# An even layer planned with new ranks and a new clock model, its queries stacked for the score products, and an odd layer with its first LayerNorm placed later

## The chip, the cores and the metric

The kernel runs on one core of a Trainium2 chip. The metric is the time of one execution on the device in microseconds, the median of repeated runs. The engines' short names are those of the profile: PE is TensorE's matmul stream and PEld its weight loads, DVE is VectorE, ACT is ScalarE, POOL is GpSimd, and SP is the engine that issues nearly all DMAs. "L446" is line 446 of the kernel's file.

## The reference

An encoder of two post-norm layers on x of 512 positions by 1024 features, in fp32, each layer followed by a convolutional FFN. The even layer (cut):

```
z = x @ w_in
q, k, v, u = jnp.split(z, [ATTN_WIDTH, ATTN_WIDTH + KV_WIDTH, ATTN_WIDTH + 2 * KV_WIDTH], axis=-1)
y_attn = windowed_gqa(q, k, v, sink)     # 8 heads of 64, 2 key/value heads, |t - s| <= 128, sink logits, ALiBi
y_s5 = s5_mixer(u, ...)                  # diagonal complex state space, both directions, then GELU and GLU
return jnp.concatenate([y_attn, y_s5], axis=-1) @ w_out
```

The odd layer is a bidirectional mLSTM with 8 heads of 128. Its tail, per head:

```
num = einsum('bhcts,bhcse->bhcte', s, v) + inter[..., None] * einsum('bhctd,bhcde->bhcte', q, c_in)
h = num / jnp.maximum(jnp.abs(den), jnp.exp(-m_t))[..., None]
h = h_fwd + h_bwd
mu = h.mean(-1, keepdims=True); var = jnp.mean(jnp.square(h - mu), -1, keepdims=True)
h = (h - mu) * lax.rsqrt(var + LN_EPS) * norm_g
h = h * jax.nn.sigmoid(o)
return h @ w_out
```

## The kernel before, in words

Every fp32 product is made of three: an operand is split into a high part (a copy rounded to the type fp32r) and a low part (the rest), and `mm3` (L545 to 547) multiplies high by high, low by high and high by low. `nat_tile` (L569) does the same for the products whose result has positions on the partitions.

The even layer, about the first 208 us, is not issued as it is written. The functions `e_*`, `att_*` and `s_*` record their instructions in a `Plan` as steps, with a part name each (`self.plan.part`: "att3", "in2", "pv0"), and `Plan.order` puts all steps of all engines in one order: among those that could start soonest it takes the one of the highest rank, where rank is the weighted length of the chain behind a step (`WEIGHT`, per engine) plus a number for its part (`BIAS`). To know what could start, it goes by costs of its own: `cost` for an instruction, `HOP` between engines, `TURN` between the kinds of products on TensorE, and a rule for TensorE's clock. `Plan.issue` then issues them in that order, so that all of them carry the one line L446 of the profile. What the names in a row say: `xh`, `xl` are the parts of x transposed; `t` is a pool of tiles of 512 columns (pieces of x, parts of q and k, inputs' products); `s` holds scores; `pT` transposed weights of attention; `mh`, `ml` the parts of the mixer's result; `wl` low parts of weights; `E`, `C`, `c`, `U`, `T`, `S`, `So`, `ra`, `rb`, `zx`, `Y` belong to the state space layer, which goes in four blocks of channels: input products (in0 to in3, into banks `b` from `U` and `nU`), rotations (`s_rot`, ending in `S`), output tables (`C`, two buffers), lags, output products (y0 to y3, from `So` and `U` with `C` and `T`), and act (GELU) with its parts. `U` is loaded per block by a DMA into one of two buffers.

Attention: `e_q` projects two heads' queries at once into 128 rows and keeps a high and a low tile of them. `e_kv` keeps k's parts per key head, `kh` and `kl`, each twice: once in its own 64 rows and once copied to the other 64, so that a head in either half of q finds its keys in its own rows. `att_scores` multiplies 64 rows of each with `mm3`, for 16 pairs of head and half, a range of 256 and one of 384 columns each.

The odd layer (`odd`) is issued through the scheduler of the framework as it is written, in steps per head: "q" and "k" (projections with their convolution), "1" (`m_weights`: scores of the head, multiplied by W, the decay matrices, L1541 and 1542), "2" (`m_sum`: the sums over W and v, L1555 and 1557, divided and put together as `hn`, then its LayerNorm, L1573 to 1579), "3" (`m_out`: transposes of `hn`, output gate). The order at its start is "1" of head 0, "q" of head 2, "2" of head 0, "1" of head 1, then "k" of head 2, "2" of head 1, "3" of head 0. LayerNorm's power -1/2 runs on POOL (L1577, `hrs`), which also makes the masked rows `nm` for `m_weights` (L1525) and, for 22 of the weight units, the low part `wl` (L529).

## Time and profile before

| | us |
|---|---|
| median of 3 runs | 1279.37 (1277.39 to 1280.87) |
| the profiled execution | 1279.63 |
| its span (first to last instruction) | 1277.8 |
| mean granted clock of TensorE in it | 0.986 |

The rows below come from the one profiled execution; its span lies 1.83 us under its own time. In the views by stretch, a busy time of an engine is followed by its number of instructions, and PEclk is the granted clock of TensorE as a share of full speed (1.00 is 2.4 GHz, 0.50 is 1.2 GHz). In a timeline, the time in brackets is the idle time of the engine ahead of the row, with what ended it.

### The profile page before, as it was taken

The numbers are of one execution on the slowest core, as the hardware profiler recorded it, in microseconds if no ns is written. First come the engines' busy times: TensorE is split into PE (matmuls) and PEld (weight loads), VectorE is DVE, ScalarE is ACT, GpSimd is POOL, SyncE is SP. The second block draws the span as 40 slices with busy tenths as digits, with TensorE's granted clock in tenths as the row PEclk, the third lists the DMA queues.
The fourth block names the chain that finished last, engine by engine and source line by source line (L and its number), as shares of the span: only waits on it lengthen the run. The fifth ranks groups of instructions, "written<-read, shape, count | busy, mean of one in ns | idle before, by whom it ended". The sixth has DMA issues, their size and how long they took to land.

```text
span 1277.8 us, 17609 instructions
## 1 busy us (share of the span) xinstructions
PE 1243.6 (97%) x6878; PEld 1044.5 (82%) x6878; DVE 718.6 (56%) x1398; ACT 527.4 (41%) x900; POOL 139.5 (11%) x139
## 2 busy tenths in 40 slices
PE   7898999999999999999999999999999999999997
PEld 5776787888888888888888898988988888888886
DVE  7999984764442444425775647375854422544415
ACT  5346765343321243322364746553443321333301
POOL 2013510000000000000014345310000000000000
PEclk9989889999999999999999999999999999999999
DMA  8633533353333233322033232224443321433201
GB/s 252 183 106 107 171 107 102 151 167 115 95 88 99 89 109 99 99 80 86 25 117 105 82 95 76 90 66 132 129 135 100 99 88 61 148 99 97 91 28 66
DMA packets 57459, 135.31 MB, mean 106 GB/s; under 512 B 13888, under 2 KB 22928, under 8 KB 56736
## 3 DMA queue, kind: packets, MB, share of 16 engines
q1 hardware_dynamic: 57376, 134.19, 33.9%
q8 instruction: 54, 0.88, 0.3%
q14 instruction: 29, 0.24, 0.1%
HBM read 129.19 MB, written 4.98 MB: 105 GB/s over the span
## 4 chain that ended last, share of the span: by engine, by line
PE 83%; DVE 9%; DMA 3%; issue 2%; ACT 2%; SPq 1%; POOL 0%; DVEq 0%; POOLq 0%; ACTq 0%
PE b L569 23%; PE b L545 18%; PE b L546 18%; PE b L547 17%; PE b L446 4%; PE b L1555 1%; PE b L1557 1%; DVE t L446 1%; DMA t<-xT_dram 1%; DVE C L446 1%; SPq L446 1%; DMA st<-w_dram 1%; DMA zx<-DZ 1%; DVE s L446 1%; DVE wl L446 0%
## 5 line engine op out<-in xcount | busy, mean ns | idle before, releaser
L545 PE MATMUL b<-xh,wh 128*128 128x512 f32 (+1 forms) x944 | 357.6, 380 | 0.5 <-ACT xh L627 0.5
L546 PE MATMUL b<-xl,wh 128*128 128x512 f32 (+1 forms) x944 | 357.2, 379 | 0.4 <-DVE xl L628 0.3
L547 PE MATMUL b<-xh,wl 128*128 128x512 f32 (+1 forms) x944 | 357.0, 378 | 0.0
L528 ACT CAST wh<-st 128x1024 fp32r<-128x1024 f32 x175 | 183.5, 1052 | 414.5 <-DMA st<-w_dram 146.2
L529 DVE TENSOR_TENSOR wl<-st,wh 128x1024 fp32r<-128x1024 f32 x153 | 188.2, 1232 | 292.6 <-ACT wh L528 288.8
L546 PEld LDWEIGHTS b<-xl,wh 128*128 128x128 f32 x944 | 177.6, 188 | 33.6 <-DVE xl L628 1.1
L547 PEld LDWEIGHTS b<-xh,wl 128*128 128x128 f32 x944 | 177.6, 188 | 33.3
L545 PEld LDWEIGHTS b<-xh,wh 128*128 128x128 f32 x944 | 177.1, 188 | 33.4 <-ACT xh L627 1.0
L569 PE MATMUL b<-wh,hh 128*128 128x512 f32 x352 | 109.3, 390 | 0.0
L569 PE MATMUL b<-wl,hh 128*128 128x512 f32 x352 | 109.2, 389 | 0.0
L569 PE MATMUL b<-wh,hl 128*128 128x512 f32 x352 | 109.2, 389 | 0.0
L610 POOL TENSOR_TENSOR lnrs<-lnsq,mhalf 128x1 f32<-128x1 f32 x16 | 9.7, 606 | 836.1 <-DVE lnsq L609 836.1
L569 PEld LDWEIGHTS b<-wh,hl 128*128 128x128 f32 x352 | 66.1, 188 | 13.8
L569 PEld LDWEIGHTS b<-wl,hh 128*128 128x128 f32 x352 | 66.1, 188 | 13.7
L569 PEld LDWEIGHTS b<-wh,hh 128*128 128x128 f32 x352 | 65.9, 188 | 13.5
L734 DVE TENSOR_TENSOR c<-c,b 128x512 f32<-128x512 f32 x44 | 30.2, 687 | 65.5 <-PE b L547 64.8
L733 ACT ACTIVATE c<-c 128x512 f32<-128x512 f32 x44 | 27.8, 632 | 81.0 <-DVE c L732 81.0
L529 POOL TENSOR_TENSOR wl<-st,wh 128x1024 fp32r<-128x1024 f32 x22 | 52.5, 2392 | 56.4 <-ACT wh L528 53.5
L591 DVE SCALAR_TENSOR_TENSOR x<-x,b 128x512 f32<-128x512 f32 x48 | 31.2, 684 | 43.0 <-PE b L569 39.8
L446 PE MATMUL b<-xh,wh 128*128 128x512 f32 x80 | 32.3, 408 | 7.4 <-ACT xh L446 7.4
L446 ACT ACTIVATE s<-s,m 128x384 f32<-128x384 f32 (+3 forms) x64 | 33.7, 557 | 13.2 <-DVE m L446 12.9
L607 ACT ACTIVATE lnjk<-x,lnmu 128x1024 f32<-128x1024 f32 x16 | 18.4, 1153 | 49.9 <-DVE lnmu L606 49.9
(330 smaller groups left out, 1867.5 us busy)
## 6 DMA issues: line engine op xcount, KB each, us to landing
st<-w_dram SPq DMA_DIRECT2D x192, 512.0 KB, 3.6
tb<-s5bT_dram SPq DMA_DIRECT2D x16, 256.0 KB, 4.3
zx<-DZ SPq DMA_DIRECT2D x16, 256.0 KB, 5.0
lngb<-ln_dram SPq DMA_DIRECT2D x4, 1024.0 KB, 5.6
nb<-DN SPq DMA_DIRECT2D x16, 256.0 KB, 3.8
t<-xT_dram SPq DMA_DIRECT2D x8, 256.0 KB, 5.4
T<-DK SPq DMA_DIRECT2D x32, 64.0 KB, 2.3
x<-x_dram SPq DMA_DIRECT2D x1, 2048.0 KB
```

Source lines behind the costliest of these rows:

```text
L446: getattr(getattr(nc, s.eng), s.name)(*real(s.args), **real(s.kw))
L528: nc.scalar.copy(out=h, in_=x)
L529: eng.tensor_tensor(out=l, in0=x, in1=h.bitcast(F32), op=ALU.subtract)
L545: mm(ps, lhsT=lh, rhs=rh, start=first, stop=False)
L546: mm(ps, lhsT=lh, rhs=rl, start=False, stop=False)
L547: mm(ps, lhsT=ll, rhs=rh, start=False, stop=last)
L569: mm(acc[h], lhsT=hx[:, tok], rhs=wx[:, 512 * h:512 * h + 512], start=a, stop=b)
L591: self.nc.vector.scalar_tensor_tensor(out=xr, in0=xr, scalar=scale, in1=acc[h], op0=ALU.mult, op1=ALU.add, **kw)
L607: nc.scalar.activation(out=jk, in_=x, func=AF.Square, bias=mu, accum_out=sq)
L733: nc.scalar.activation(out=c, in_=c, func=AF.Gelu_apprx_tanh)
L734: nc.vector.tensor_tensor(out=c, in0=c, in1=pg, op=ALU.mult)
L1555: nc.tensor.matmul(pn[:, 0:130], lhsT=Ws[j][:, i - j, :], rhs=va[:, j, h % 2, 0:130], start=j == 0, stop=j == i)
```

## The change

Five things are edited. First, the table of ranks (`BIAS`, `WEIGHT`), of which the diff shows a line. Second, what the planner believes of TensorE: the costs of a turn between kinds of products, and its rule for the clock, which now counts columns instead of costs, with other bounds. Third, `e_kv`: the copy of k's low part to the other 64 rows moves from VectorE to ScalarE. Fourth, `e_q` and `att_scores`: instead of a high and a low tile of both heads, there are two tiles, one per head, with the head's high part in its own 64 rows and its low part in the other 64. Since `kh` holds the same keys in both halves, one product over 128 rows gives high by high and low by high together, and a second one over 64 rows with `kl` the rest. Fifth, in the odd layer the LayerNorm of `m_sum` becomes a function of its own, `m_norm`; it follows `m_sum` at once for all heads but head 0, whose LayerNorm now comes after "1" of head 1.

```diff
-BIAS = {"act0": -6545, "act1": -21250, "act2": -210, "act3": 869, "att0": 17397, "att1": -8738, "att2": 28314,
+BIAS = {"act0": -15215, "act1": -28185, "act2": -8486, "act3": 16119, "att0": 13532, "att1": -8687, "att2": 14400,
...
-WEIGHT = dict(tensor=564.3857644116506, vector=0.10825561484528345, scalar=16158.12505118024, gpsimd=1.858247289234654, sync=0.07166590488045835, form=59.399941409009884)
+WEIGHT = dict(tensor=6921.451288255964, vector=0.09311711213243236, scalar=23712.06630937233, gpsimd=391.23029167485606, sync=0.7156231908378619, form=4.460256149243044)
...
-    TURN = {"FR": 0.22, "FT": 0.18, "RF": 0.15, "RT": 0.05, "TF": 0.145, "TR": 0.105}
+    TURN = {"FR": 0.23, "FT": 0.2, "RF": 0.15, "RT": 0.1, "TF": 0.19, "TR": 0.105}
...
+            wide = math.prod(args[1].shape[1:]) if name == "transpose" else math.prod(kw["rhs"].shape[1:])
+            s.act = wide / 2400 * (2 if name == "transpose" else 1 if kw["rhs"].f32r else 4)
...
-                busy += cost
+                busy += s.act
...
-            nc.vector.tensor_copy(out=kl[kv][other, :], in_=kl[kv][own, :].bitcast(F32))
+            nc.scalar.copy(out=kl[kv][other, :], in_=kl[kv][own, :].bitcast(F32))
...
-        qh = self.t(ap, [P, S], "t", F32R, bufs=NT)
-        ql = self.t(ap, [P, S], "t", F32R, bufs=NT)
-        nc.scalar.activation(out=qh, in_=pq, func=AF.Copy, scale=0.125)
-        nc.vector.scalar_tensor_tensor(out=ql, in0=pq, scalar=0.125, in1=qh.bitcast(F32), op0=ALU.mult, op1=ALU.subtract)
-        return qh, ql
+
+        q = [self.t(ap, [P, S], "t", F32R, bufs=NT) for _ in range(2)]
+        for r in range(2):
+            own, other = slice(64 * r, 64 * r + 64), slice(64 - 64 * r, 128 - 64 * r)
+            nc.scalar.activation(out=q[r][own, :], in_=pq[own, :], func=AF.Copy, scale=0.125)
+            nc.vector.scalar_tensor_tensor(out=q[r][other, :], in0=pq[own, :], scalar=0.125, in1=q[r][own, :].bitcast(F32), op0=ALU.mult, op1=ALU.subtract)
+        return q
...
-            self.mm3(pt[:, 0:n], qh[rows, ds128(j)], ql[rows, ds128(j)], kh[rows, keys], kl[rows, keys], True, True)
+
+            nc.tensor.matmul(pt[:, 0:n], lhsT=q[par][:, ds128(j)], rhs=kh[:, keys], start=True, stop=False)
+            nc.tensor.matmul(pt[:, 0:n], lhsT=q[par][rows, ds128(j)], rhs=kl[rows, keys], start=False, stop=True)
...
+        return hn, st, mv, rs
+
+    def m_norm(self, hn, st, mv, rs):
+        nc = self.nc
+        v = nc.vector
         for i in range(4):
             v.bn_stats(out=st[:, i, :], in_=hn[:, i, :])
...
                 hn[h] = self.m_sum(mp, h, Ws.pop(h), va[h // 2])
+                if h > 0:
+                    hn[h] = self.m_norm(*hn[h])
...
         step("2", 0)
         step("1", 1)
+        hn[0] = self.m_norm(*hn[0])
```

How the order moves is shown at three places. The first is the start of SP's queue, from its first or second transfer of x on. Here `t` is a piece of x, `st` a staged weight, `KS` the small parameters of the state space layer, `tb` its tables. Before:

```order
L446 DMA t_108<-xT_dram 128x512
L446 DMA t_112<-xT_dram 128x512
L446 DMA KS_115<-s5s_dram 128x96
L446 DMA t_118<-xT_dram 128x512
L446 DMA bias_122<-bias_dram 128x384
L446 DMA t_124<-xT_dram 128x512
L446 DMA ident_72<-ident_dram 128x128
L446 DMA pv_73<-pv_dram 128x256
L446 DMA tb_128<-s5bT_dram 128x1x512
L446 DMA DG_130<-dg_dram 80x256
L446 DMA t_132<-xT_dram 128x512
L446 DMA t_134<-xT_dram 128x512
```

After (rows 2 to 13 of SP's order; row 1 is the first piece of x):

```order
L451 DMA t_97<-xT_dram 128x512
L451 DMA st_101<-w_dram 128x1024
L451 DMA st_105<-w_dram 128x1024
L451 DMA t_109<-xT_dram 128x512
L451 DMA t_112<-xT_dram 128x512
L451 DMA t_115<-xT_dram 128x512
L451 DMA t_118<-xT_dram 128x512
L451 DMA KS_122<-s5s_dram 128x96
L451 DMA bias_124<-bias_dram 128x384
L451 DMA t_126<-xT_dram 128x512
L451 DMA ident_72<-ident_dram 128x128
L451 DMA t_129<-xT_dram 128x512
```

Ahead of these stand the two weights and two pieces of x in the order before, and one piece of x in the order after. All eight pieces are issued by the 13th place now, by the 16th before.

The second place is TensorE's, where the input products of block 2 begin (`U_1507` and `U_1641` are that block's U). `b<-t,t` are score products (the parts of k first, of q second), `b<-ident,s` transposes of scores, `b<-pT,t` the products with v, `b<-So,C` output products of block 0 (into `b_1391` in the order after). Before:

```order
L446 MATMUL b_1545<-t_484,t_1044 128x384
L446 MATMUL b_1550<-t_484,t_1044 128x256
L446 MATMUL b_1545<-t_515,t_1044 128x384
L446 MATMUL b_1550<-t_515,t_1044 128x256
L446 MATMUL b_1545<-t_484,t_1066 128x384
L446 MATMUL b_1550<-t_484,t_1066 128x256
L446 MATMUL b_1561<-ident_72,s_1374 128x128 x3
L446 MATMUL b_1430<-pT_1548,t_944 64x128 x3
L446 MATMUL b_1576<-U_1507,t_371_1180 64x64 x2
```

After:

```order
L451 MATMUL b_1567<-pT_1630,t_789 64x128 x3
L451 MATMUL b_1391<-So_1106,C_432 64x64
L451 MATMUL b_1663<-ident_72,s_1509 128x128 x2
L451 MATMUL b_1391<-So_1106,C_432 64x64
L451 MATMUL b_1567<-pT_1665,t_789 64x128 x2
L451 MATMUL b_1391<-So_1106,C_432 64x64
L451 MATMUL b_1681<-ident_72,s_1509 128x128 x3
L451 MATMUL b_1391<-So_1106,C_432 64x64
L451 MATMUL b_1694<-t_499,t_1344 128x384
L451 MATMUL b_1699<-t_499,t_1344 128x256
L451 MATMUL b_1694<-t_514,t_1344 128x384
L451 MATMUL b_1702<-U_1641,t_371_1103 64x64 x2
```

A score has two products where it had three, and the last output products of block 0 (`b_1391`) now stand right ahead of block 2's input, where they were over some rows earlier; the new U takes the buffer that these read.

The third place is VectorE's, in the odd layer, from the LayerNorm of head 0 (`hst`, `hmv`, `hrs`, `hn`) to the products with W of head 1. Before:

```order
L1573 BN_STATS hst_6104<-hn_6103 128x6 x4
L1575 BN_AGGR hmv_6105<-hst_6104 128x2 x4
L1541 TENSOR_TENSOR W_6137<-W_6137,b_6138 128x512
L1576 TENSOR_SCALAR hrs_6106<-hmv_6105 128x4
L1542 TENSOR_TENSOR W_6137<-W_6137,b_6138 128x128
L1579 TENSOR_SCALAR hn_6103<-hn_6103,hmv_6105,hrs_6106 128x128 x4
L1541 TENSOR_TENSOR W_6149<-W_6149,b_6150 128x384
L1542 TENSOR_TENSOR W_6149<-W_6149,b_6150 128x256
L1541 TENSOR_TENSOR W_6161<-W_6161,b_6162 128x256
L1542 TENSOR_TENSOR W_6161<-W_6161,b_6162 128x384
L1541 TENSOR_TENSOR W_6173<-W_6173,b_6174 128x128
L1542 TENSOR_TENSOR W_6173<-W_6173,b_6174 128x512
```

After (the same functions stand some lines lower in the changed file):

```order
L1550 TENSOR_TENSOR W_6099<-W_6099,b_6100 128x128
L1549 TENSOR_TENSOR W_6111<-W_6111,b_6112 128x384
L1550 TENSOR_TENSOR W_6111<-W_6111,b_6112 128x256
L1549 TENSOR_TENSOR W_6123<-W_6123,b_6124 128x256
L1586 BN_STATS hst_6080<-hn_6079 128x6 x3
L1550 TENSOR_TENSOR W_6123<-W_6123,b_6124 128x384
L1549 TENSOR_TENSOR W_6135<-W_6135,b_6136 128x128
L1586 BN_STATS hst_6080<-hn_6079 128x6
L1588 BN_AGGR hmv_6081<-hst_6080 128x2 x4
L1550 TENSOR_TENSOR W_6135<-W_6135,b_6136 128x512
L1589 TENSOR_SCALAR hrs_6082<-hmv_6081 128x4
L1592 TENSOR_SCALAR hn_6079<-hn_6079,hmv_6081,hrs_6082 128x128 x4
```

The statistics, and above all the four normalising steps of `hn` that wait for POOL's `hrs`, stood between the first and the second W; they now stand behind all four.

## Rows read from the trace of the kernel before

**Rows 1.** The page's first part: busy time, share of the span, instructions.

```profile
PE 1243.6 (97%) x6878; PEld 1044.5 (82%) x6878; DVE 718.6 (56%) x1398; ACT 527.4 (41%) x900; POOL 139.5 (11%) x139
```

**Rows 2.** By stretch: length, then PE, PEld, DVE, ACT, POOL, PEclk, DMA, GB/s.

```profile
0.00:20.00 20.00, 11.16 (x37) 8.24 (x38) 12.46 (x43) 9.87 (x13) 7.41 (x15) 1.00 0.92 302
20.00:192.60 172.60, 160.01 (x1493) 129.52 (x1492) 160.12 (x436) 99.15 (x223) 40.50 (x58) 0.91 0.47 137
65.00:75.00 10.00, 10.00 (x103) 9.04 (x102) 7.86 (x19) 3.72 (x11) 1.25 (x1) 0.54 0.30 91
155.00:170.00 15.00, 15.00 (x92) 12.51 (x93) 10.71 (x22) 7.41 (x20) 6.49 (x11) 0.62 0.28 85
208.00:684.60 476.60, 474.27 (x2284) 399.59 (x2283) 238.73 (x353) 170.37 (x234) 17.80 (x17) 1.00 0.33 104
```

**Rows 3.** Timeline at the planned part's end: start us, us, engine, line, operation, count.

```profile
182.54 1.28 ACT L446 ACT_TABLE_LOAD   x1
...
191.30 1.29 DVE L446 TENSOR_TENSOR S<-S,ra 128x512 f32<-128x512 f32 x2
...
198.70 0.50 PE L446 MATMUL b<-xh,ml 128*128 128x512 f32 x1
...
208.19 0.39 PE L545 MATMUL b<-t,wh 128*128 128x512 f32 x1
```

**Rows 4.** Timeline of VectorE: two of its waits in the planned part.

```profile
15.98 0.69 DVE L446 TENSOR_TENSOR xl<-t,xh 128x512 fp32r<-128x512 f32 x1 [1.56 <-ACT xh L446]
...
166.93 2.48 DVE L446 TENSOR_TENSOR C<-bc,b 128x512 f32<-128x512 f32 x4 [3.21 <-PE b L446]
```

**Rows 5.** Timeline of TensorE: waits ahead of two stretches, and score products around one.

```profile
64.23 0.90 PE L446 MATMUL b<-t,t 64*128 64x384 f32 x2 [1.79 <-DVE t L446]
...
146.53 1.15 PE L446 MATMUL b<-t,t 64*128 64x384 f32 x6
...
152.98 1.11 PE L446 MATMUL b<-pT,t 128*64 128x128 f32 x6 [2.52 <-ACT pT L446]
...
161.22 1.97 PE L446 MATMUL b<-t,t 64*128 64x384 f32 x6
```

**Rows 6.** VectorE from 0 to 208 by form: busy us, mean ns; idle us before.

```profile
L446 DVE TENSOR_TENSOR t<-zx,tb 128x512 f32<-128x512 f32 x32 | 23.0, 745 | 2.9 <-DMA zx<-DZ 1.9 <-PE b L446 1.0
...
L446 DVE SCALAR_TENSOR_TENSOR t<-b,t 128x512 fp32r<-128x512 f32 x4 | 2.7, 678 | 0.0
...
L446 DVE TENSOR_TENSOR t<-b,t 64x512 fp32r<-64x512 f32 x2 | 1.4, 684 | 0.0
...
L446 DVE CAST t<-t 64x512 fp32r<-64x512 f32 x2 | 0.8, 422 | 0.0
```

**Rows 7.** Timeline of TensorE: the products of m_sum, head 0 and then head 1.

```profile
684.89 1.06 PE L1557 MATMUL b<-va,W 128*128 128x130 f32 x8
685.78 0.61 PE L1555 MATMUL b<-va,W 128*128 128x130 f32 x4
...
697.52 0.39 PE L1557 MATMUL b<-va,W 128*128 128x130 f32 x2
...
700.56 0.61 PE L1555 MATMUL b<-va,W 128*128 128x130 f32 x4
```

**Rows 8.** Timeline of POOL and VectorE at the LayerNorm of head 0.

```profile
693.65 1.02 POOL L1577 TENSOR_TENSOR hrs<-hrs,mhalf 128x4 f32<-128x4 f32 x1 [5.48 <-DVE hrs L1576]
...
694.71 3.09 DVE L1579 TENSOR_SCALAR hn<-hn,hmv,hrs 128x128 f32<-128x128 f32 x4 [0.95 <-POOL hrs L1577]
...
695.06 2.65 POOL L1525 TENSOR_TENSOR nm<-nb,msk 128x512 f32<-128x512 f32 x2 [0.39 <-ACT W L1536]
...
698.44 2.36 POOL L529 TENSOR_TENSOR wl<-st,wh 128x1024 fp32r<-128x1024 f32 x1 [0.72 <-ACT wh L528]
```

**Rows 9.** The line of the normalising steps: ns min/median/max, first and last start.

```profile
L1579 DVE TENSOR_SCALAR hn<-hn,hmv,hrs x32: 341/346/1418, 694.7 to 870.4; 128x128 f32<-128x128 f32 x32
```

**Rows 10.** The page's DMA issues: KB each, us from issue to landing.

```profile
T<-DK SPq DMA_DIRECT2D x32, 64.0 KB, 2.3
```

More of the change, by code (lines that the diff above doesn't have):

```diff
@@ L189 @@
 class Step:
-    __slots__ = ("eng", "name", "args", "kw", "deps", "users", "cost", "size", "table", "port", "form", "first", "claims", "roots", "prio", "rank", "part", "end", "left", "at")
+    __slots__ = ("eng", "name", "args", "kw", "deps", "users", "cost", "size", "table", "port", "form", "act", "first", "claims", "roots", "prio", "rank", "part", "end", "left", "at")
 class PlanEngine:
@@ L206 @@
     HOP = dict(tensor=0.22, vector=0.16, scalar=0.2, gpsimd=0.16, sync=0.1)
-    TURN = {"FR": 0.22, "FT": 0.18, "RF": 0.15, "RT": 0.05, "TF": 0.145, "TR": 0.105}
+    TURN = {"FR": 0.23, "FT": 0.2, "RF": 0.15, "RT": 0.1, "TF": 0.19, "TR": 0.105}
     SAME = dict(tensor=0.0, vector=0.13, scalar=0.14, gpsimd=0.1, sync=0.0)
+    phase = 0.0
     def __init__(self, net):
@@ L271, in record @@
         s.port = self.port(s)
-        s.form = None
+        s.form, s.act = None, 0.0
         if eng == "tensor":
+            wide = math.prod(args[1].shape[1:]) if name == "transpose" else math.prod(kw["rhs"].shape[1:])
+            s.act = wide / 2400 * (2 if name == "transpose" else 1 if kw["rhs"].f32r else 4)
             s.form = "T" if name == "transpose" else "R" if kw["rhs"].f32r else "F"
@@ L412, in order @@
             if s.eng == "tensor":
-                while int(start / 3.413) > window:
-                    warm = busy > (0.36 if warm else 0.73) * 3.413
+                while int((start + self.phase) / 3.413) > window:
+                    warm = busy > (0.52 if warm else 0.46) * 3.413
                     window, busy = window + 1, 0.0
                 cost *= 1.0 if warm else 2.0
-                busy += cost
+                busy += s.act
             clock[s.eng] = start + cost
@@ L847, in att_scores @@
         rows = slice(64 * par, 64 * par + 64)
-        qh, ql = q
         kh, kl = self.kd[0][kv], self.kd[1][kv]
```

30 rows, old and new, of the table BIAS are left out of this document.

## The prediction

> **What bounds the kernel now.** I read the page's head first: TensorE is busy 97% of the span [rows 1], and VectorE, ScalarE and POOL behind it far less. That average hides a stage that is ruled otherwise, so the stretches come next. From 208 us on TensorE is at work for 474.27 of 476.6 us at full clock [rows 2]; whatever the even layer ends earlier is passed on one for one. In the planned part (0 to 208 us) the longest gapless work is VectorE's. It is busy 12.46 us of the first 20 and 160.12 of the next 172.6, up to the end of the last rotation at 192.6 us [rows 2, 3]: 7.5 and 12.5 us of idle time are all that a better order could take out there. TensorE shows as many busy microseconds, but at a mean granted clock of 0.91, and partly with work that nobody waits for. From the last rotation on TensorE leads again: y3, and then 41 matmuls of 512 columns from 198.70 on without a gap, until GLU starts at 208.19 [rows 3].
>
> VectorE's idle time is then looked for in lumps. One is at the start: 1.56 us for the last low part of x [rows 4]. The others lie in two stretches in which TensorE was granted about half its clock, the 1.2 GHz level, for most of the time: 2.14 us of 65 to 75 (0.54) and 4.29 of 155 to 170 (0.62; the clock comes back in its last third) [rows 2]; the largest single wait in them is 3.21 us, for y1 to leave a buffer of C [rows 4]. Ahead of both stretches TensorE had stood still, 1.79 us for a low part on VectorE and 2.52 us for pT on ScalarE, and six score matmuls of 384 columns took 1.97 us in the second of them against 1.15 before it [rows 5].
>
> **The change, part by part.** The sum goes against the profiled execution's 1279.63 us (span 1277.8 and 1.83 around it), 0.26 above the median.
>
> *The stacked q and the copy of k-low.* A q now has two high and two low parts of 64 rows in place of one of each with 128 rows. On VectorE 64 rows cost what 128 do: 684 and 678 ns [rows 6], in a row at a pitch of (2.48 - 0.68)/3 = 0.60 us [rows 4, 6]. Four q's give four more: +2.4. Two CASTs of 422 ns go to ScalarE, at a pitch some 0.08 shorter: -0.7. The order moves two of act's low parts (`t<-s,t`) from ahead of the last rotation to behind it; they then fall into VectorE's waits of the tail: -1.2. Net **+0.5** on VectorE's path; if the four all fall into idle lumps it is -1.9, and if the two low parts only press elsewhere, +1.7. ScalarE gains four more copies and two CASTs, some 3 to 4 us, and is busy 99.15 of 172.6 [rows 2]: I cost that at nothing, hidden by its 73 idle microseconds; where scores wait for it, it costs up to one copy, 0.5 us, a q. TensorE loses 32 of the 96 score matmuls: 16 x 1.15/6 = 3.1 us for the wide ones and about two thirds of it for the narrow ones, 5 us at full clock and, by 1.97 in place of 1.15, up to 8.7 at half. It is work off the path except in the two half-clock stretches, and is counted there.
>
> *The start.* The new order issues all eight pieces of x by the 13th transfer in place of the 16th, the two pieces that stand first ahead of the weights. The wait of 1.56 us for the last of them [rows 4] should go, and the two weights' low parts and x's follow more densely. VectorE has little idle time from there to 60 us, so it passes on. I take **-2.2**, between 0 (it waits for something else in the crowded first 20 us, where the DMA engines are busy 0.92 [rows 2]) and -3.
>
> *The middle.* 2.14 + 4.29 = 6.4 us of idle time lie in the half-clock stretches and just behind. The new ranks reorder all of it, and in the new order y1 ends, by the rows that stand ahead, well before VectorE writes the third C, so that the 3.21 us wait has no reason in its old place. What granted clock the new order gets the order doesn't say. Bounds: 0 (a like lump elsewhere) and -6.4 (all go). I take the half, **-3.2**, since one of the two waits ahead of a spell (on a low part of k or q) has a direct cause in what is changed and the other hasn't.
>
> *The tail.* Five of the 41 matmuls of 512 columns move ahead of y3: 5 x (208.19 - 198.70)/41 = 0.23, so -1.15. Against it ScalarE now does the table load of 1.28 us, two gelus and two CASTs between the last rotation's copy and Y's [rows 3], about 0.9 us more than y3 takes, and mh's last copy stands behind Y. Net **-0.3**, between -1.3 and +0.5.
>
> *The odd layer.* TensorE's eight products of head 0 at L1557 run 0.89 us (684.89 to 685.78); head 1's take 3.04 (697.52 to 700.56), part of it waiting for the W's [rows 7]. The difference, 2.15 us, is VectorE's: four normalising steps of head 0 took 3.09 us from 694.71, where 346 ns is the median of one [rows 8, 9]; they stood beside nm on POOL (2.65 us from 695.06). The change puts the W products of head 1 ahead of them. The stall at 697.52 goes: -2.15. What is late next is hn of head 0. Its pow now stands behind both nm on POOL (695.06 + 2.65 = 697.7), and adds 1.02 as it did at 693.65 [rows 8]; the normalising then lies beside wl on POOL (2.36 us), and if that stretches it as nm did, it ends at 698.8 + 3.1 = 701.9. TensorE, 2.15 us earlier, reaches the transposes of hn at about 701.5. So up to 0.5 is given back: **-1.7**, bounds -2.15 and 0 (the transposes wait as long as the products did). The Trainium skill, SBUF — State Buffer, section "Who interferes with whom", says that VectorE and GpSimd share a pair of ports by an exclusive lock, held for a whole instruction, and that the loser stands still. The trace agrees as far as it shows it: beside nm the slowest of the 32 took 1418 ns [rows 9]. By that rule, if wl took the lock first, the normalising would wait for wl's end at 701.2 and finish near 702.6, and this term would be -1.1 in place of -1.7.
>
> Sum: +0.5 - 2.2 - 3.2 - 0.3 - 1.7 = -6.9; 1279.6 - 6.9 = **1272.7 us**.
>
> **The rivals.** *A, all lumps go.* Two thirds of the score matmuls on TensorE and the clock held through both stretches take the whole 6.4; with -1.3 in the tail and -1.9 in the odd layer: 1279.6 - (2.2 + 6.4 + 1.3 + 1.9 - 0.5) = 1268.3. For it: the waits ahead of both spells are single ones. Against it: the order has many more of them (VectorE also waits 1.9 us for zx and 1.0 for TensorE at the head of in [rows 6]).
>
> *B, the start and the middle don't move.* The lumps have the same sum in other places, and the start's gain ends at the next transfer: only the odd layer and half the start are left: 1279.6 + 0.5 - 1.7 - 1.1 = 1277.3. For it: zx's 1.9 us is a transfer's wait that new ranks don't shorten by themselves. Against it: the two large waits have causes that the order moves.
>
> *C, a new spell of half clock at block 2's input.* In the new order those products stand behind the end of y0, since U's DMA waits for a buffer that y0 reads, and SP issues in order. VectorE has 25 rows ahead of block 2's rotation from the scores of head 6 on: fourteen of 512 columns at 0.60 = 8.4, four score reductions at 0.5 and small ones, 11.6 us. TensorE's rows there (four score matmuls, some 60 products of 64 columns, the transposes) are an estimated 6.7 us at full clock: enough. At half clock it would be 13.4, and some 3 for U's transfer (T's take 2.3 to land [rows 10], and it has a place in the queue): VectorE would stand still for 13.4 + 3 - 11.6 = 4.8 us. Were the clock still low through the lags, up to y1, the same count gives 23.7 us on VectorE against 27.3 and U's 3, and each further wait of this kind adds like sums; I take 13 as its upper end. Time: 1272.7 + 4.8 = 1277.5, up to 1285.7; it decides for slower once it costs over 6.9 + 3.8 = 10.7. For it: two such spells in the profile, each behind a wait of 1.8 to 2.5 us [rows 5]. Against it: 6.7 against 11.6 is room, and fewer score matmuls leave less work in it. The Trainium skill, TensorE: Matmul & The Clock Gate, "HAM oscillation", tells of a kernel in which idle gaps between bursts cost the full clock each time; by it every new gap of y0 would make C likelier. The rows show it only behind waits of 1.8 us and more, and none that long is forced here by the order, so I leave C's chance at that.
>
> **How the numbers follow.** 0.3% (3.8 us) is about what a measurement of this kernel can tell from no change, so faster is below 1275.5 and slower above 1283.2. The forecast has 0.52 (its own range 1268.5 to 1275.5), A 0.15, B 0.13; C has 0.20, of it 0.08 within 0.3% and 0.12 above. That gives faster 0.67, same 0.21, slower 0.12. The range of 8 in 10 leaves out the upper part of C and the lower edge of A: 1264.5 to 1283.
>
> **What would show it.** VectorE: at least 1 us less idle time in the first 20 us; the last rotation ending at 187 to 188.5 in place of 192.6; busy time 1.7 us above before. Granted clock: no stretch of 10 us near 0.5 that VectorE waits in; with one at block 2's input C is right. GLU's first matmul 5 us earlier than 208.19. Odd layer: the products of head 1 in 0.9 us in place of 3.04, without a wait for W, and the normalising no longer ahead of W; a wait of TensorE's transposes for hn below 0.5. The prediction is wrong if the last rotation ends later than 191, or if what is gained by 208 is lost again before the FFN.

## The result and the profile after

| | before | changed |
|---|---|---|
| median of 4 runs each, us | 1278.69 (1277.39 to 1280.87) | 1293.01 (1292.70 to 1295.39) |
| ratio, 95% interval | | 1.0106 (1.0088 to 1.0124) |
| span of the profiled execution | 1277.8 | 1293.5 |
| last rotation of the planned part ends | 192.6 | 209.1 |
| GLU's first matmul starts | 208.19 | 224.70 |

The change is slower by 1.1%; the prediction was 1272.7 us, faster by 0.5%, and its range ended at 1283. The page's head looks like [rows 1]:

```profile
PE 1247.7 (96%) x6846; PEld 1037.5 (80%) x6846; DVE 726.3 (56%) x1400; ACT 530.5 (41%) x906; POOL 137.8 (11%) x139
```

The stretches say where the time went (columns as in [rows 2]):

```profile
0.00:20.00 20.00, 9.36 (x29) 6.72 (x29) 11.58 (x27) 8.01 (x11) 7.87 (x15) 1.00 0.85 277
20.00:209.12 189.12, 166.74 (x1480) 126.37 (x1480) 167.34 (x453) 101.34 (x227) 38.90 (x58) 0.91 0.44 129
72.30:82.50 10.20, 10.20 (x66) 7.08 (x67) 3.31 (x11) 2.51 (x8) 0.00 (x0) 0.50 0.25 71
209.12:226.00 16.88, 15.38 (x147) 11.73 (x147) 5.55 (x8) 11.18 (x16) 0.00 (x0) 1.00 0.19 48
224.70:701.50 476.80, 474.31 (x2285) 399.49 (x2284) 239.37 (x355) 170.76 (x236) 17.58 (x17) 1.00 0.33 104
```

The FFN is what it was (474.31 of 476.8 against 474.27 of 476.6 us in [rows 2]), and from the last rotation to GLU it is 15.6 us in both. All of the loss, 16.5 us in this pair of profiles, arises before the last rotation ends, less about 1 us that the odd layer gives back. (The profiled execution of the changed kernel is the slowest of its four; by the ratio the loss is 13.6 us.) In that part VectorE is busy 178.9 us (172.6 before) and idle 30.2 (20.0 before): +6.3 and +10.2. The mean granted clock is 0.91 as before; at half clock are 34.1 us (30.7 before).

The idle part: VectorE's waits by what ended them, total, number of times, longest, up to the last rotation. Before:

```profile
DVE wl L446 <- ACT wh L446: 4.7, 1, 4.7
DVE C L446 <- PE b L446: 3.2, 1, 3.2
DVE t L446 <- DMA zx<-DZ: 1.9, 2, 1.5
DVE xl L446 <- ACT xh L446: 1.7, 2, 1.6
DVE s L446 <- PE b L446: 1.5, 4, 0.6
DVE ra L446 <- PE b L446: 1.3, 1, 1.3
...
DVE t L446 <- PE b L446: 1.0, 2, 0.6
```

After:

```profile
DVE s L451 <- PE b L451: 6.7, 6, 2.4
DVE t L451 <- PE b L451: 5.5, 4, 2.8
DVE wl L451 <- ACT wh L451: 5.2, 3, 3.4
DVE xl L451 <- ACT xh L451: 3.8, 1, 3.8
DVE t L451 <- DMA zx<-DZ: 2.2, 4, 0.7
DVE C L451 <- PE b L451: 1.3, 1, 1.3
```

The wait for y1 ahead of C, the largest of [rows 4], has shrunk as forecast (3.2 to 1.3). But VectorE now waits 13.5 us for TensorE in all (7.0 before). Half of it stands in one half-clock stretch; TensorE's timeline there, then VectorE's:

```profile
70.56 0.81 PE L451 MATMUL b<-t,t 128*128 128x384 f32 x2 [1.03 <-DVE t L451]
...
72.17 2.24 PE L451 MATMUL b<-t,t 128*128 128x256 f32 x4
...
75.17 2.33 PE L451 MATMUL b<-t,t 128*128 128x256 f32 x4
```

```profile
73.22 0.48 DVE L451 CUSTOM_DVE_ANT_0 s<-b,bias,ns 128x256 f32<-128x256 f32 x1 [0.66 <-PE b L451]
...
74.45 0.62 DVE L451 CUSTOM_DVE_ANT_0 s<-b,bias,ns 128x384 f32<-128x384 f32 x1 [0.74 <-PE b L451]
...
76.31 0.48 DVE L451 CUSTOM_DVE_ANT_0 s<-b,bias,ns 128x256 f32<-128x256 f32 x1 [0.69 <-PE b L451]
...
79.58 0.69 DVE L451 TENSOR_TENSOR t<-zx,tb 128x512 f32<-128x512 f32 x1 [2.79 <-PE b L451]
82.29 0.69 DVE L451 TENSOR_TENSOR t<-zx,tb 128x512 f32<-128x512 f32 x1 [2.01 <-PE b L451]
```

TensorE had waited 1.03 us for q's low part and then had thin work; from 72.3 it is granted half its clock, and scores and block 0's input products come out at half speed just where VectorE needs them: 6.9 us of waits. How much of these the clock makes, and how much the order, is measured below (*c_after*).

The busy part: four of POOL's seven low parts of weights (named `xl` or `wl`, from a staged weight `st`) lie beside a step of VectorE that lasts as long as POOL's. VectorE's steps, then POOL's:

```profile
118.19 2.62 DVE L451 TENSOR_TENSOR E<-E,e 128x256 f32<-128x256 f32 x1
...
125.61 2.84 DVE L451 TENSOR_TENSOR ra<-ra,rb 128x512 f32<-128x512 f32 x1
...
148.21 2.58 DVE L451 TENSOR_TENSOR e<-E,ph 128x256 f32<-128x256 f32 x1
...
161.59 3.44 DVE L451 TENSOR_TENSOR C<-C,c 128x512 f32<-128x512 f32 x2
```

```profile
118.05 2.47 POOL L451 TENSOR_TENSOR xl<-st,xh 128x1024 fp32r<-128x1024 f32 x1 [0.27 <-ACT xh L451]
125.56 2.35 POOL L451 TENSOR_TENSOR xl<-st,xh 128x1024 fp32r<-128x1024 f32 x1
...
147.96 2.56 POOL L451 TENSOR_TENSOR wl<-st,wh 128x1024 fp32r<-128x1024 f32 x1
...
161.96 2.53 POOL L451 TENSOR_TENSOR wl<-st,wh 128x1024 fp32r<-128x1024 f32 x1 [4.84 <-ACT wh L451]
```

A step of 128x256 takes 0.42 us elsewhere in this trace (E at 68.43), one of 128x512 0.69 (t at 79.58). Before, only two such steps are stretched (beside POOL's low parts at 121.95 and 155.34). All that are stretched read two tiles in SBUF. That agrees with the Trainium skill, SBUF — State Buffer, "Who interferes with whom": a VectorE instruction with two SBUF inputs contends with a GpSimd one that reads SBUF, under an exclusive lock, and the order of issue decides which of them blocks.

POOL's low parts of x do the same in the first 20 us. VectorE's own four low parts of x, by form, before and after, then q's low parts after, and act's low parts before (after, none stands ahead of the last rotation):

```profile
L446 DVE TENSOR_TENSOR xl<-t,xh 128x512 fp32r<-128x512 f32 x4 | 3.6, 889 | 1.7 <-ACT xh L446 1.7
```

```profile
L451 DVE TENSOR_TENSOR xl<-t,xh 128x512 fp32r<-128x512 f32 x4 | 5.3, 1354 | 3.8 <-ACT xh L451 3.8
...
L451 DVE SCALAR_TENSOR_TENSOR t<-b,t 64x512 fp32r<-64x512 f32 x8 | 5.5, 688 | 0.7 <-ACT t L451 0.6
```

```profile
L446 DVE TENSOR_TENSOR t<-s,t 128x512 fp32r<-128x512 f32 x2 | 1.4, 680 | 0.0
```

So of the 6.3 us more that VectorE is busy, four steps held up by the weights' low parts in place of two are some 4, the low parts of x 1.7, and the change's own steps 0.6: q's parts 5.5 in place of 2.7, less two CASTs (0.8) and two of act's low parts (1.4).

The odd layer's products of head 0 and of head 1 and what comes behind them, on TensorE, VectorE and POOL:

```profile
701.58 1.06 PE L1565 MATMUL b<-va,W 128*128 128x130 f32 x8
...
714.21 1.06 PE L1565 MATMUL b<-va,W 128*128 128x130 f32 x8
715.10 0.61 PE L1563 MATMUL b<-va,W 128*128 128x130 f32 x4
...
727.92 1.01 PE L1600 MATMUL b<-ident,hn 128*128 128x128 f32 x4 [0.68 <-DVE hn L1592]
```

```profile
715.46 3.13 DVE L1592 TENSOR_SCALAR hn<-hn,hmv,hrs 128x128 f32<-128x128 f32 x4 [1.14 <-POOL hrs L1590]
```

```profile
715.39 2.35 POOL L534 TENSOR_TENSOR wl<-st,wh 128x1024 fp32r<-128x1024 f32 x1
```

The stall of [rows 7] is gone: from head 0's products to head 1's it is 13.52 us (701.58 to 715.10) in place of 15.67 (684.89 to 700.56), the 2.15 forecast.

### The profile page after: what moved, and what is told of

Same layout as the page of the kernel before. It is cut to its first block, busy times and chain, and to the rows that moved or that the text cites. A ratio compares the mean times of both kernels' runs of the same rounds, so it can differ in the third digit from the quotient of the medians.

```text
span 1293.5 us, 17556 instructions
## 1 busy us (share of the span) xinstructions
PE 1247.7 (96%) x6846; PEld 1037.5 (80%) x6846; DVE 726.3 (56%) x1400; ACT 530.5 (41%) x906; POOL 137.8 (11%) x139
## 4 chain that ended last, share of the span: by engine, by line
PE 79%; DVE 10%; DMA 5%; issue 3%; ACT 2%; SPq 0%; POOL 0%; DVEq 0%; POOLq 0%; ACTq 0%
PE b L574 21%; PE b L551 17%; PE b L550 17%; PE b L552 17%; PE b L451 3%; DMA st<-w_dram 2%; PE b L1565 1%; PE b L1563 1%; DMA zx<-DZ 1%; DVE t L451 1%; DVE C L451 1%; DVE wl L534 1%; DVE rb L451 1%; DVE ra L451 1%; DVE E L451 1%
## 5 line engine op out<-in xcount | busy, mean ns | idle before, releaser
L574 PEld LDWEIGHTS b<-wh,hh 128*128 128x128 f32 x352 | 65.9, 188 | 13.6
L739 DVE TENSOR_TENSOR c<-c,b 128x512 f32<-128x512 f32 x44 | 30.2, 687 | 65.7 <-PE b L552 64.2
```

Source lines behind the costliest of these rows:

```text
L574: mm(acc[h], lhsT=hx[:, tok], rhs=wx[:, 512 * h:512 * h + 512], start=a, stop=b)
L739: nc.vector.tensor_tensor(out=c, in0=c, in1=pg, op=ALU.mult)
```

## The experiments

The theory after the profile had three parts: the order, not the new tiles, carries most (theory O); in it, POOL holds VectorE up more often (theory P, also "port"); and VectorE waits in spells of half clock (theory K). The rivals were that q's new parts cost it (theory Q), or the late start, and that the spells only go with waits that the order makes anyway (rival W). Times are ratios to the kernel before on the same chip, with their 95% interval, and the end of the last rotation in the profile. That end is of one execution: e_odd, e_oddact and the kernel before have the same planned part and end it at 193.5, 190.9 and 192.6.

| kernel | ratio | rotation ends |
|---|---|---|
| e_odd | 0.9991 (0.9976 to 1.0007) | 193.5 |
| e_oddact | 1.0001 (0.9983 to 1.0018) | 190.9 |
| f_qk | 1.0031 (1.0010 to 1.0053) | 196.8 |
| f_order | 1.0092 (1.0062 to 1.0121) | 199.1 |
| e_oldranks | 1.0067 (1.0046 to 1.0089) | 200.6 |
| f_start | 1.0170 (1.0144 to 1.0196) | 213.5 |
| f_start2 | 1.0098 (1.0068 to 1.0128) | 203.9 |
| n_before | 0.9962 (0.9947 to 0.9977) | 187.6 |
| n_after | 1.0021 (1.0007 to 1.0035) | 197.1 |
| h_odd | 0.9985 (0.9973 to 0.9997) | 194.3 |
| c_odd | 0.9971 (0.9957 to 0.9985) | 189.3 |
| c_after | 1.0040 (1.0023 to 1.0056) | 197.6 |
| nc_odd | 0.9960 (0.9944 to 0.9976) | 187.9 |
| nc_after | 1.0005 (0.9992 to 1.0018) | 193.7 |
| c_qk | 1.0062 (1.0046 to 1.0078) | 202.0 |
| b_best | 0.9988 (0.9974 to 1.0001) | 191.1 |
| c2_odd | 0.9978 (0.9963 to 0.9993) | 190.7 |

**The parts of the change.** To part the order from the tiles, the planner's order is replaced by a list, in f_qk that of before, in f_order that of the changed kernel:

```diff
     def order(self):
         steps = self.steps
+        if len(steps) == len(FIXED):
+            return [steps[i] for i in FIXED]
```

*e_odd*, the kernel before with `m_norm` alone. Expected: 

> The kernel before with the odd layer's move alone (the LayerNorm of head 0 behind the W products of head 1). Theory O (the even layer's new order makes the loss) and theory Q (the stacked q and k-low's copy make it) expect the same here: TensorE's waits for W at head 1's products go (-2.2 us), and about 1.1 us comes back where head 1's transposes wait for hn, because VectorE's normalising of head 0 now lies beside wl on POOL and ahead of head 1's denominators: 1.1 us faster than before, span 1276.7. If the give-back were an accident of the changed even layer: 2.2 us faster.

*f_qk*, the new tiles of q and k in the old order. Expected: 

> The kernel before with the stacked q, the two products per score and k-low's copy on ScalarE, in the order of before, instruction by instruction (each new pair of half-height steps stands where the one step stood; the one product over 128 rows stands where the first of three stood). Theory O: the work itself is nearly neutral, between 3 us faster (32 products fewer) and 2.5 us slower (four more steps of 0.6 us on VectorE, two copies fewer): 1276 to 1281. Theory Q: the half-height steps and the copies on ScalarE hold up the scores, and most of the 14 us is here: 1288 or more.

*f_order*, the new order with the old tiles and the old odd layer. Expected: 

> The kernel before with the instruction order of the changed kernel, but with its own q (one high and one low tile), three products per score, k-low's copy on VectorE and the odd layer of before. Theory O: nearly the whole loss is here, 12 to 17 us slower than before: 1291 to 1296. Theory Q: within 3 us of before, 1276 to 1282.

The odd layer moves the median by about 1 us, inside its interval. The order alone is +11.8 us, just below theory O's 12 to 17; its profile is the fastest of its four executions. In it VectorE is busy 178.8 us up to the last rotation, as in the changed kernel (178.9): with the old tiles, the order alone brings nearly all of VectorE's added busy time. The tiles in the old order are +4.0, above theory O's 2.5 and far from theory Q. They have a cause that the order of before makes. There, TensorE met the first score product when only ScalarE's high part of q was there; in f_qk that product also reads VectorE's low part. TensorE before, then VectorE and TensorE in f_qk:

```profile
60.81 0.62 PE L446 MATMUL b<-t,t 64*128 64x384 f32 x2 [0.54 <-ACT t L446]
```

```profile
63.85 1.41 DVE L529 SCALAR_TENSOR_TENSOR t<-b,t 64x512 fp32r<-64x512 f32 x2
```

```profile
64.59 1.30 PE L529 MATMUL b<-t,t 128*128 128x384 f32 x2 [4.99 <-DVE t L529]
```

Before, TensorE waits 0.54 us here and then 1.79 at 64.23 for the low part [rows 5], with products between the two; in f_qk it waits 4.99 at once, 2.7 us more, and is at half clock behind it. The changed kernel's own order leaves more room (1.03 at 70.56 above), so +4.0 is not what the tiles cost there.

*e_oldranks*, the changed kernel with the old `BIAS` and `WEIGHT`. Expected: 

> The changed kernel with the ranks of before: the new clock model and turns, the new parts of q and k and the new odd layer stay, the planner makes its own order. Theory R (the searched ranks made the order bad, the model did not): the order comes near the old one, +1.5 to +4 for the parts of q and k, -1.1 in the odd layer, ratio 1.000 to 1.002. Theory M (the new model plans badly by itself): ratio 1.006 or more.

Theory M: with the old ranks, the new clock rule and turns (and the new tiles, which the planner also has to place) already give +8.6 us; the searched ranks add some 5. Here the last rotation's end says too little: GLU starts 21.7 us behind it, at 222.28. Which of turns, bounds, column count and new tiles does it was not tried apart.

**The start.** In the changed kernel the third weight's products stand between those of the first two units, and TensorE waits 3.27 us for that weight at 21.94. *f_start* moved them and the casts back. Expected: 

> The changed kernel with the start of its order repaired: the first two weights ahead of x on SP, ScalarE and VectorE, and on TensorE the products of the third weight behind the last ones of the first two (they stood between them, and TensorE waited 3.27 us for that weight's cast at 18.7 us); all else as in the changed order. Theory carried (VectorE's lag of 3 to 4 us at 25 us is passed on to the end, and the half-clock spell at 21 to 28 us goes): 3 to 5 us faster than the changed kernel, 1288 to 1290. Theory absorbed (the later waits of VectorE for TensorE at 70 to 83 and 134 to 146 us swallow it): within 1 us of the changed kernel, 1292 to 1294.

It is 8.2 us slower than the changed kernel and says nothing of the start, since it made a wait of its own: ScalarE's copy of a bank stood ahead of one that VectorE needed. VectorE in f_start:

```profile
42.10 2.48 DVE L534 TENSOR_TENSOR C<-bc,b 128x512 f32<-128x512 f32 x4 [8.78 <-ACT b L534]
```

*f_start2* is a smaller repair without that. Expected: 

> A smaller repair of the changed kernel's start (the first repair made a wait of its own: 8.8 us of VectorE for a copy on ScalarE that stood behind TensorE's delayed units). The first two weights ahead of x on SP, ScalarE and VectorE as there; on TensorE only the fifteen rows from the first product of the third weight on are reordered, the products of the first two weights first; the first unit's copy and its DMA ahead of the next weight's. Theory carried (the start's lag of 3 to 4 us on VectorE goes to the end): 1288 to 1290. Theory absorbed (the waits of VectorE at 70 to 83 us come anyway): 1292 to 1294.

Its ratio is that of the changed kernel within its interval of about 4 us, as the theory "absorbed" has it. But its profile doesn't show that theory's way: the same five waits come, nearly as long as in the changed kernel, and VectorE leaves the last of them at 78.32 in place of 82.29 and GLU starts at 219.70 in place of 224.70, 4 and 5 us earlier. The lead is passed on; of it 3.0 us are left in the span. Those are two single executions, the slowest of four of the changed kernel and the fastest of four of this one. So the start is at most a small part of the loss, and whether it costs nothing or some 3 to 4 us stays open.

**POOL.** In *n_before* and *n_after* the orders stay, and POOL's low parts are not computed:

```diff
-            eng.tensor_tensor(out=l, in0=x, in1=h.bitcast(F32), op=ALU.subtract)
+            if self.plan and pool:
+                eng.memset(l.bitcast(F32), 0.0)
+            else:
+                eng.tensor_tensor(out=l, in0=x, in1=h.bitcast(F32), op=ALU.subtract)
```

Expected of n_before: 

> The kernel before, in its own order, with the seven low parts of weights that POOL makes in the even layer left out: POOL writes zeros in their place and reads nothing (about 1 us in place of 2.4), so that the low half of these weights is missing in the result. Theory port (a VectorE step with two operands in SBUF stands still while such a POOL step runs): two of the seven stretched a VectorE step by 2.2 us in the profile of before, so 4.4 us faster than before, 1274 to 1277 against 1279 to 1281. Theory other waits (what VectorE loses to POOL is swallowed by its later waits for TensorE): within 1.5 us of before.

Expected of n_after: 

> The changed kernel, in its own order, with the same seven low parts left out (POOL writes zeros and reads nothing; the low half of these weights is missing in the result). Theory port: four of the seven stretched a VectorE step by 2.1 to 2.2 us each in the profile of the changed kernel, 8.7 us, so 7 to 9 us faster than the changed kernel, 1284 to 1286. Theory other waits: within 2 us of the changed kernel, 1291 to 1294.

They are 4.9 and 10.9 us below their own kernels (1.0106 to 1.0021 for the second): theory P holds. VectorE's busy time up to the last rotation falls by 6.0 us (172.6 to 166.6) and by 9.0 (178.9 to 169.9), so POOL holds it up 3 us longer in the new order. The times differ by 6, but less time at half clock went with it in both (medians 33.3 to 22.9 us in the old order, 36 to 28 in the new), so not all of the 6 is POOL's.

*h_odd* puts the two that met VectorE before on VectorE (`ENG_W`, "g" to "v" for two units), with the new odd layer. Expected: 

> The kernel before with the odd layer's new order and two of POOL's seven low parts of weights (those that ran at 121.95 and 155.34 beside a stretched step of VectorE) on VectorE, in the same order. Theory P (POOL's step holds up VectorE's step by its own length): -1.1 in the odd layer and 2 x (2.2 - 1.2) = 2.0 on VectorE's path, -3 us, ratio 0.9976. Rival: POOL's other five low parts, moved in time, meet VectorE's steps instead: -1, ratio 0.999.

It gained 0.8 us over e_odd, less than 2.0, within the intervals. Its trace shows the rival at work: a VectorE step `t<-zx,tb` at 144.73 now lasts 2.22 us beside another of POOL's low parts (144.05, 2.35 us); in the kernel before the longest step beside that part (143.13) took 0.87.

**The clock.** *c_odd* and *c_after* add products on TensorE ahead of rows that waited in front of a spell. They write where the next product starts anew, so nothing else changes (`FILL` gives for a step of the plan how many stand ahead of it, and whether they fill the whole bank):

```diff
             for s in done:
+                n, whole = FILL.get(index[id(s)], (0, False))
+                if n:
+                    keys = real(self.net.xh)[:, 0, :] if s.part == "u2" else real(self.net.kd[0][1])
+                    to = s.args[0].root.place() if whole else real(s.args[0])
+                    if not whole:
+                        keys = keys.bitcast(F32)
+                    for _ in range(n):
+                        nc.tensor.matmul(to, lhsT=keys[:, 0:to.shape[0]], rhs=keys[:, 0:to.shape[1]], start=True, stop=True)
```

Expected of c_odd: 

> The kernel before with the odd layer's new order, and 44 products on TensorE added whose results are overwritten at once: they stand ahead of rows that waited in front of the four spells of half clock (7 of 512 columns ahead of the first score's wait at 64.23, 3 ahead of the lags at 97.33, 6 ahead of the transposes and scores at 99.52, 6 at 126.48, 11 ahead of pT's wait at 152.98). Theory K (a us at half clock costs 0.3 us, as the runs of the kernel before among themselves show): of 30.7 us at half clock most go, the last rotation ends near 186, time -1.1 - 0.3 x 20 to 25 = -7 to -8.5, ratio 0.994. Rival W (the waits come from the order, and the spells only go with them): ratio 0.999 as the odd layer alone, or up to 1.001 where the added products stand in the way.

Expected of c_after: 

> The changed kernel with 64 such products, ahead of the waits at 21.94 (13), 54.74 (11), the scores at 70.56 to 75 (9), and pT's waits at 133.37 (12) and 153.54 (9). Theory K: of 34.1 us at half clock 20 to 25 go, the last rotation ends near 201 to 203, time 6 to 7.5 us below the changed kernel's, ratio 1.005, and VectorE's waits at 73 to 82.5 (6.9 us) shrink to below 2. Rival W: they stay, ratio 1.010 as without the products.

(The products that the two expectations list place by place are 33 and 54; their totals, and "38" further down, were miscounted.) By stretch, c_after:

```profile
0.00:197.60 197.60, 174.95 (x1584) 133.24 (x1584) 178.76 (x478) 108.80 (x238) 46.49 (x73) 1.00 0.51 152
```

its waits of VectorE for TensorE, and the steps that waited at 73 to 82.5 us in the changed kernel:

```profile
DVE t L463 <- PE b L463: 2.6, 2, 1.5
...
DVE s L463 <- PE b L463: 1.8, 3, 0.8
...
DVE C L463 <- PE b L463: 0.8, 1, 0.8
```

```profile
71.23 0.48 DVE L463 CUSTOM_DVE_ANT_0 s<-b,bias,ns 128x256 f32<-128x256 f32 x1 [0.81 <-PE b L463]
...
72.44 0.62 DVE L463 CUSTOM_DVE_ANT_0 s<-b,bias,ns 128x384 f32<-128x384 f32 x1 [0.72 <-PE b L463]
...
75.54 0.69 DVE L463 TENSOR_TENSOR t<-zx,tb 128x512 f32<-128x512 f32 x1 [1.50 <-PE b L463]
77.37 0.69 DVE L463 TENSOR_TENSOR t<-zx,tb 128x512 f32<-128x512 f32 x1 [1.14 <-PE b L463]
```

The clock is full throughout this profile, VectorE is as busy as in the changed kernel (178.8 and 178.9 us), but its idle time is 18.8 us in place of 30.2; its waits for TensorE fell from 13.5 to 5.2. The median fell by 8.4 us (1.0106 to 1.0040): theory K. Less of it than forecast comes from the stretch at 73 to 82.5: there 4.2 of the 6.9 us of waits are left at full clock (forecast: below 2), so the order makes most of them, as rival W has it. More went further on: three waits for scores behind pT's wait at 133.37, in the changed kernel 1.51, 2.42 and 0.63 us at 136.73, 141.53 and 145.00, shrank to one of 0.28. In the order of before, c_odd gained 2.6 us over e_odd (0.9991 to 0.9971), about as much as its interval and far from the 6 to 7.5 forecast; some 17 us of half clock went, 20 to 25 were expected. This agrees with a spell costing what VectorE waits in it, not a fixed rate.

*c2_odd* tested that rate, with more products ahead of the two spells that c_odd still had. Some of these overwrite one group's input products in blocks 0 and 1, so the numbers that it computes are others, with the same instructions behind them. Expected: 

> The kernel before with the odd layer's new order, the 38 added products, and 14 more, ahead of the two spells of half clock that were left with them (48 to 51 and 78 to 86 us, behind idle times of TensorE of 0.90 and 1.77): 6 at the head of block 0's input products, 8 in block 1's. Theory K: of 10 us at half clock most go, -2 to -3 us, 1274.5, ratio 0.995. Rival W: VectorE waits little in those two spells, and the added products stand ahead of its inputs: 0.997 as without them, or up to 0.998.

Median time at half clock fell from 16.6 to 10.2 us, and the time did not fall (0.9978): rival W here.

**What is left with the clock held.** *nc_odd* and *nc_after* are c_odd and c_after without POOL's low parts. Expected of nc_odd: 

> The kernel before with the odd layer's new order and the added products that held the clock, with POOL's seven low parts of weights in the planned part filled with zeros in place of the difference (the low parts are left out of the products). In the trace with those low parts three of them stood beside a step of VectorE stretched to their length (122.9, 154.3, 157.8). Theory P (POOL holds VectorE up): 3 x 2.1 less, one of them partly beside a wait, -4 to -6 us against that kernel, 1272, ratio 0.9935. Rival: those steps only stand where VectorE would wait anyway: -1 us.

Expected of nc_after: 

> The changed kernel with its added products and POOL's seven low parts left out in the same way. Four of them stood beside a stretched step (112.9, 120.3, 133.1, 140.2), at 1285.4 us. Theory P: 4 x 2.1 = -8, 1277, ratio 0.9975; what is left of the 8.4 us between the two kernels with the clock held is then 5 us. If the whole rest of the loss were POOL's, it would be 1273 to 1274.

POOL's toll at full clock is 1.4 us in the old order and 4.5 in the new one, less than 4 and 8, though VectorE's busy time falls by 6.4 and 9.3. Waits absorb the rest: VectorE's idle time rises by 5.0 us (15.1 to 20.1) and 5.4 (18.8 to 24.2). To the end of the last rotation, nc_odd and then nc_after:

```profile
0.00:187.90 187.90, 171.00 (x1580) 137.47 (x1581) 167.83 (x478) 109.47 (x237) 35.50 (x73) 0.97 0.54 159
```

```profile
0.00:193.70 193.70, 175.23 (x1583) 134.48 (x1583) 169.50 (x478) 108.82 (x238) 35.93 (x73) 0.99 0.52 155
```

With both tolls taken away the new order is still 5.8 us behind (0.9960 to 1.0005), as these rows show: VectorE is busy 1.7 us more and idle 4.1 us more (24.2 against 20.1). Of the busy time the change's own steps are 0.7, with act's two low parts behind the last rotation; its low parts of x, beside POOL's, are 1.8, and others take 0.8 less. The idle time is again waits for TensorE, now at nearly full clock: 8.3 us against 4.0.

*c_qk* is c_odd with the new tiles. Expected: 

> The order of before with the added products and the new odd layer, and the new parts of q and k in it: what these cost with the clock held. By VectorE's busy time (four more parts, two casts less): +1.7 on 1277.0, 1278.7, ratio 0.9985. Rival: +4, as without the added products, for the waits of scores for ScalarE's copies: 1281, ratio 1.000.

At 1.0062 it misses both forecasts, and it says little of the tiles: the wait of f_qk stands in it too, and the added products behind that wait run at half clock (3.26 us for seven) and delay the scores further.

*b_best* should join both causes. Expected: 

> A version meant to beat both kernels: before with the odd layer's new order, the added products that held the clock, and on VectorE the three of POOL's low parts that stood beside its stretched steps (122.9, 154.3, 157.8). 3 x (2.1 - 1.2) = 2.7 at most, with two of the three moved into the two at 154 and 157: -2 against 1277.0, 1275, ratio 0.9955. Rival: moved in time, others of POOL's steps meet VectorE's: 1277, 0.997.

It is not better than c_odd; the rival holds: another of POOL's low parts (142.36) now lies beside a VectorE step of 2.68 us (142.60). The best version found that leaves nothing out is c_odd: the kernel before with the new odd layer and 33 idle products on TensorE, 0.9971 (0.9957 to 0.9985).

**The odd layer once more.** *e_oddact* is e_odd with head 0's normalising on ScalarE. Expected: 

> The kernel before with the odd layer's move, and with head 0's four normalising steps on ScalarE (scale and bias per row; one more small step on VectorE) in place of VectorE, so that neither wl on POOL stretches them nor head 1's denominators stand behind them. If VectorE's 3.1 us there make the give-back of 1.1 us: about 2.1 us faster than before in the trace from 697 to 730 us, 1 us more than the move alone. If ScalarE's steps hold up its own queue (th and the W exponentials stand behind them): no more than the move alone, 1.1 us, or less.

It gains nothing over e_odd: from head 0's products to head 2's it takes 39.76 us (e_odd 38.33, before 39.27). The held-up step has only moved on: VectorE's normalising of head 1 now meets POOL's next `wl` (710.18, 2.40 us) and lasts 3.15 us from 709.51, in e_odd 1.12, and head 1's last transpose waits 1.96 us for it at 712.72.

## Why the prediction was wrong

The loss in parts, each from two ratios (times 1280 us): with the clock held on both sides, the changed kernel gains 8.4 us and the order of before 2.6, so spells account for 5.9; without POOL's low parts, 4.5 against 1.4, so POOL for 3.1; left are 5.8; the odd layer gives -1.2. The sum, 13.6, is 1.06%; it comes out so by the way the differences are taken, and is no check of the parts. Each ratio has an interval of about 2 us to either side, so a part made of four ratios has some 4: the spells and what is left are clear of zero, POOL's 3.1 by its times alone is not, but VectorE's busy time shows the same 3 us.

*The middle (-3.2): the step that failed.* "Bounds: 0 (a like lump elsewhere) and -6.4 (all go)" took the old idle time for the most that a new order could have. What was said of the old lump was right: the wait for y1 fell from 3.2 to 1.3. But the waits for TensorE grew from 7.0 to 13.5 us, all idle time up to the last rotation from 20.0 to 30.2; and with the clock held and POOL's seven low parts out, the waits for TensorE are still 8.3 against 4.0. The bound should have had a plus side of the same size as the minus side. Why the new clock model and ranks choose this order was not found.

*A term was missing.* POOL's hold on VectorE was weighed for one place in the odd layer. The planned part has seven POOL steps of 2.4 us of that kind, and VectorE leads there; which of its two-input steps they meet is set by the order. Its toll rose by 3 us at full clock, and by 6 with the spells, not all of it POOL's. POOL's four low parts of x added 1.7 us of the same kind at the start.

*The tiles (+0.5, at most +1.7).* On VectorE's busy time the size was right: its own steps give +0.6 to +0.7, with act's two low parts behind the last rotation as forecast. Overlooked was the new dependence: a score's first product now needs VectorE's low part, where it needed only ScalarE's copy. The stall is 4.99 us in the old order (f_qk; 0.54 and 1.79 before) and 1.03 in the new one, there with a spell behind it.

*The start (-2.2).* x came first, but the weights' casts came later, and VectorE's idle time in the first 20 us rose from 7.5 to 8.4 us; its low parts of x took 1.7 us more. "Passes on" is not refuted: in the profile of f_start2 a lead of 4 us outlasts the waits at 70 to 78 us, though its median gains no more than its interval.

*The tail (-0.3).* 0.0: 15.6 us from last rotation to GLU in both.

*The odd layer (-1.7).* The mechanism was right, the size smaller. The stall's 2.15 went in full. Then the normalising lay 3.13 us beside POOL's wl, as the sentence from the Trainium skill had it, and the give-back came not at head 0's transposes, which did not wait, but at head 1's (0.68 us for hn, and slower by 0.4). From head 0's products to head 2's, e_odd takes 38.33 us in place of 39.27: -0.9. By that rule the forecast was -1.1.

*Rival C* had the kind of loss (spells of half clock in which VectorE waits), but not the place: the worst is at block 0's input, and the total time at half clock hardly rose (30.7 to 34.1 us). It was priced as one event, with 0.12 above no change; three causes of 3 to 6 us each went one way. And "only behind waits of 1.8 us and more" was too few rows: the spell at 72.3 us stands behind a wait of 1.03.

## What to carry to other kernels

A new order of a stage that one engine leads is a new draw of all its waits: the waits of the old order bound what can be won, not what can be lost, and the range should be about symmetric. Look for the POOL steps that read SBUF beside the leading VectorE's two-input steps, and count them before and after. Where an engine's thin stretch ends in half clock and the leader then waits for it, products that fill its idle time can pay; where nobody waits, they don't.

## What the runs showed of the hardware

- The time of one kernel's runs goes with how long TensorE is at half clock: 23 runs of the kernel before on one chip have 22.9 to 54.0 us of it (twice the granted clock's shortfall times the span) and spans of 1274.5 to 1286.0, with a slope of 0.30 us per us (r = 0.90). Removing it by added products gave 0.34 (8.4 us for some 25) in the new order, 0.16 (2.6 for 17) in the old one, and nothing in c2_odd: the slope between runs is no price.
- 54 products whose results are thrown away took 8.4 us off the changed kernel (1.0106 to 1.0040), though its TensorE is busy 96% of the span.
- A POOL subtraction of 1024 columns (2.4 us) held up even a VectorE step of 16x64 to 2.44 us (155.35, before); steps that read a bank of TensorE's results beside it kept their time (0.68 us for c<-bc,b at 138.85, beside POOL's from 138.16).
